# Three Strassen products in layer A: where the top-k rounds, the key and value splits, the next queries' load and the last rotation stand

## The chip, the cores and the metric

The kernel runs on one core of one Trainium2 chip. The metric is the device time of one execution, in microseconds; the time before is the median of three runs, 1827.25 us (1826.81 to 1828.52).

## The reference, cut to what matters

The reference is a decoder trunk of two layers over 512 positions of width 2048, in float32. Layer A is the one that the change touches:

```python
def mixer_a(x, w_in, w_o, positions):
    proj = x @ w_in
    q, k, v, gate, iq, ik, iw = jnp.split(proj, SPLITS_A, axis=-1)
    q = partial_rope(q.reshape(b, s, N_HEADS_A, HEAD_DIM), positions, ROT_DIM)
    k = partial_rope(k.reshape(b, s, N_KV_A, HEAD_DIM), positions, ROT_DIM)
...
    def block_fn(args):
        dots = jnp.einsum('bqhd,bsd->bqhs', iqb, ik)
        iscore = jnp.einsum('bqhs,bqh->bqs', jax.nn.relu(dots), iwb) * idx_scale
        iscore = jnp.where(causal[None], iscore, -jnp.inf)
        _, idx = lax.top_k(iscore, n_sel)
        ksel = jax.vmap(lambda kk, ii: kk[ii])(k, idx)
        vsel = jax.vmap(lambda vv, ii: vv[ii])(v, idx)
        logits = jnp.einsum('bqngd,bqknd->bqngk', qg, ksel) * (HEAD_DIM ** -0.5)
        wts = jax.nn.softmax(logits, axis=-1)
        o = jnp.einsum('bqngk,bqknd->bqngd', wts, vsel)
...
    return (o * jax.nn.silu(gate)) @ w_o
```

There are 16 query heads of width 128 in four groups, each group sharing one key and value head. An indexer scores all earlier positions for each query, and the attention sees only the 128 best of them (n_sel is min(256, 512 / 4)). Layer B is a stick-breaking attention over keys and values that are computed once. After each layer come a layer norm and a gated embedding.

## The kernel before, in words

Everything is kept transposed: a tile has 128 features on the partitions and positions along the free axis. Every float32 product is three matmuls (lines 147 to 149, `mm3`): each operand is split into a high part, rounded to the matmul's own format, and a low part that holds the rest. `split` makes them: ScalarE copies the high part (`wh`, `sh`, `xh`, `qh`, `kh`, `vh`, `ph`), VectorE subtracts for the low part (`wl`, `sl`, and so on). A weight streams from memory into a raw tile, is split, and is then read by TensorE. Buffers for parts are few (three each of wh, wl, sh and sl), so both engines work a few products ahead of TensorE and no further.

Some products are done by Strassen's scheme with seven products instead of eight. Their weights need sums of quarters, which VectorE adds before the split. The seven results stand in seven of the eight PSUM banks, and `combine` puts them together: ScalarE copies one into `u` and two more into the result, VectorE adds the rest. The next pass begins in the free bank and then needs the others one by one, so TensorE waits if `combine` empties them late.

Layer A runs in this order. First come the indexer's queries and keys and the query groups 0 to 2, with the indexer's scores between them. Then come the keys and values, in three stages of products (m2 and m4; m1 and m7; m6, m5 and m3). Then come three Strassen passes (`n` is 0, 1 and 2): the gates of groups 1 and 2 and the queries of group 3. While the second pass runs, `turn_keys` transposes the keys on TensorE. Last comes attention: four head groups `g`, each in four blocks `i` of 128 queries, beside the plain products of the gates of groups 0 and 3, whose steps fill TensorE's time between the blocks' own matmuls.

The order of work is written out by hand in three ways.

- `bg` is a queue of small pieces of work, above all for VectorE. `pumped` and `pumped_at` take one piece from it at chosen steps of a product. In the order of VectorE's instructions it stands at that place.
- Top-k is done in rounds of VectorE: `more` finds the eight largest values of a row (MAX8) and replaces them (MATCH_REPLACE8); sixteen rounds find 128, and a `mask` of two operations then turns the rest into additive masks `am`. For the last block of queries five pieces are still undone when the indexer's scores are through: four rounds and the mask. They are taken off `bg` into the list `rounds` (line 1067) and put back in the second Strassen pass (line 1134).
- In attention, `beside` (called with the strings in `ORDERS` and `OTHERS`) writes each block as letters: S is one head's scores and softmax of the next block, T four transposes of the probabilities, V the product with the values, f one step (three matmuls) of a gate product. The list `waiting` holds small pieces, and each f takes one from it (`one_waiting`), behind the newest exponential and the newest scaling of a softmax. Scores and transposes share three spare PSUM banks.

The tiles `F[0]` to `F[3]` hold the query groups and lend their room. When attention begins, `F[1]` holds the keys (`Kf`) and `F[2]` the values (`Vf`), while the queries of groups 1 and 2 wait in device memory (`held_q`). A load of group 1 into `F[1]` (line 1314) can start only when the last of the four `split_key` has read the keys, and the load into `F[2]` (line 1313) when the last `split_value` has read the values. Both are issued from GpSimd's queue, which works in order. The queries of group 1 are then split (`following_query`). Group 3 is finished by three sums of `combine` that are left over (`late`), by packing the rows to be rotated (`pack_rows`, four DMAs), and by the rotation itself (`turns`, four pieces of VectorE that end with four DMAs back).

Of the kernel before, what the change touches and what calls it, by code (L numbers as in the profile page):

```python
# [18 lines left out]
T = 512  # L19
# [32 lines left out]
def steps(gen, n):  # L52
    for _ in range(n):
        next(gen, None)
# [23 lines left out]
def trunk_kernel(  # L78
# [16 lines left out]
    nc = tc.nc  # L95
# [63 lines left out]
    F = [top.tile([128, 4, T], F32, name=f"f{c}") for c in range(4)]  # L159
# [251 lines left out]
    bg = deque()  # L411

    def paced(fn, *args):
        was, pinned[0] = pinned[0], True
        fn(*args)
        pinned[0] = was
# [409 lines left out]
    waiting = deque()  # L826
    held_g = {g: dram.tile([128, 4, T], F32, name=f"heldg{g}") for g in (1, 2)}
    held_q = [dram.tile([128, 4, T], F32, name=f"heldq{g}") for g in range(3)]
# [213 lines left out]
    def pair(first, name):  # L1042
        return [bank((first + j) % 8, name) for j in range(2)]
# [30 lines left out]
    for j in range(2):  # L1074
        paced(lambda: act.activation(c21[:, j], m4[j], AF.Copy, scale=-1.0))

    m1, m7 = pair(1, "m1"), pair(7, "m7")
    run(pumped(gemm_quarters(kv, ((half(0, 0), m1), (summed(1), m7))), 6))
    for j in range(2):
# [18 lines left out]
    steps(gemm, 2)  # L1098
    for j in range(2):
        paced(dve.tensor_tensor, u[:, j], u[:, j], m6[j], ALU.add)  # L1100
    steps(gemm, 2)
    for j in range(2):
        paced(act.activation, c12[:, j], m5[j], AF.Copy)
# [26 lines left out]
    for n, g in enumerate((1, 2, 3)):  # L1130
        M = product_banks(1 - n)
        gemm = pumped_at(gemm_s(items, C3A, M), PUMPS[n])
        if n == 1:
            bg.extend(rounds)
            steps(gemm, 40)
            for k in range(4):
                steps(gemm, 16)
                turn_keys(k)
        if n == 2:
            nc.gpsimd.dma_start(F[0][:, 0:2], held_q[0][:, 0:2])  # L1140
            bg.extend(turned_rows(KP, lambda g: key_rows(g, slice(0, 32))))
        run(gemm)
        drain()
        if n < 2:
            bg.extend(combine(None, M, lambda i: quarter(F[3], i), u[:, :, 0:H]))
            bg.extend(lambda j=j: act.activation(F[3][:, j], F[3][:, j], AF.Silu) for j in range(4))
            bg.append(lambda g=g: nc.gpsimd.dma_start(held_g[g], F[3]))
# [17 lines left out]
    def split_value(t):  # L1165
        split(*V[t], Vf[:, t])

    def split_key(g):
        split(*(k.rearrange("p (t s) -> p t s", t=4) for k in K[g]), key_rows(g))
# [14 lines left out]
    def following_query(g, h):  # L1184
        Q[g + 1, h] = split_query(g + 1, h)

    def scores(g, i):
        w = 128 * (i + 1)
        s = slice(i * 128, w)
        sm = pb.tile([128, 4, 4], F32, name="sm", tag="sm", bufs=2)  # L1190
        P[i] = pb.tile([128, 4, 384 + 128 * (i % 2)], F32, name="p", tag=f"p{i % 2}")
        for h in range(4):
            ps = spare("s")
            mm3(ps[:, :w], [q[:, s] for q in Q[g, h]], [k[:, :w] for k in K[g]], True, True)
            p = P[i][:, h, :w]
            least, rs, ri = (sm[:, h, j : j + 1] for j in range(3))
            with tc.issue_after(newest["soft" if h == 0 else "first"].ins) if "soft" in newest else ExitStack():
                newest["first"] = dve.tensor_tensor_reduce(p, ps[:, :w], am[i], -HSCALE, -GONE, ALU.add, ALU.min, least)
            newest["exp"] = act.activation(p, p, AF.Exp, bias=least, scale=-1.0, accum_out=rs)
            dve.reciprocal(ri, rs)  # L1200
            newest["soft"] = dve.tensor_scalar(p, p, ri, None, ALU.mult)
            if i == 3 and g < 3 and h == 3:
                if g == 1:
                    waiting.extend([lambda: None] * 5)
                waiting.extend(lambda h=h: following_query(g, h) for h in range(g == 1, 4))
            if (g, i, h) == (3, 3, 3):
                waiting.extend(lambda n=n: split(*plain(n), fblock(n)) for n in (0, 8, 1, 9))
            yield
            if i == 3 and g == 1 and h == 1:
                following_query(1, 0)  # L1210
# [61 lines left out]
    def beside(order, following, values):  # L1272
# [18 lines left out]
    OTHERS = {  # L1291
# [10 lines left out]
    def first_query(h):  # L1302
        Q[0, h] = split_query(0, h)

    for n, piece in enumerate((
        late.popleft(), late.popleft(), lambda: split_key(0), *(lambda h=h: first_query(h) for h in range(2)),
        lambda: split_value(0), *(lambda h=h: first_query(h) for h in range(2, 4)),
    )):
        steps(fill, 2 if n > 2 else 1)
        paced(piece)  # L1310
    waiting.extend((
        *late, lambda: split_value(1), lambda: split_key(1), lambda: split_value(2), lambda: split_key(2),
        lambda: split_value(3), lambda: nc.gpsimd.dma_start(F[2], held_q[2]), lambda: split_key(3),
        lambda: nc.gpsimd.dma_start(F[1], held_q[1]), pack_rows, *turns,
    ))
    first = scores(0, 0)
    beside("S f S f S f S fff", first, None)
# [939 lines left out]
```

## Time and profile before

| what | value |
|---|---|
| median of three runs | 1827.25 us |
| the profiled execution | 1829.19 us |
| its span, first to last instruction | 1827.1 us |
| TensorE busy | 1812.9 us, 99% of the span |
| VectorE busy | 1544.9 us, 85% |
| ScalarE busy | 1052.9 us, 58% |
| chain that ended last, share of TensorE | 96% |
| mean granted TensorE clock | 0.998 |

The table is from the page of the profiled execution. Busy time tells little here on where time is lost, since TensorE is busy nearly always; the views to read are the waits of TensorE (who waited for whom) and then the timeline around each of them. A wait for several things is put down to the one that came last. Times in a timeline count from the start of the span.

### The profile page before, as it was taken

The numbers are of one execution on the slowest core, as the hardware profiler recorded it, in microseconds if no ns is written. First come the engines' busy times: TensorE is split into PE (matmuls) and PEld (weight loads), VectorE is DVE, ScalarE is ACT, GpSimd is POOL, SyncE is SP. The second block draws the span as 40 slices with busy tenths as digits, with TensorE's granted clock in tenths as the row PEclk, the third lists the DMA queues.
The fourth block names the chain that finished last, engine by engine and source line by source line (L and its number), as shares of the span: only waits on it lengthen the run. The fifth ranks groups of instructions, "written<-read, shape, count | busy, mean of one in ns | idle before, by whom it ended". The sixth has DMA issues, their size and how long they took to land.

```text
span 1827.1 us, 28253 instructions
## 1 busy us (share of the span) xinstructions
PE 1812.9 (99%) x10231; PEld 1596.4 (87%) x10231; DVE 1544.9 (85%) x3085; ACT 1052.9 (58%) x1953; POOL 33.5 (2%) x75
## 2 busy tenths in 40 slices
PE   9999999999899999999999999999999999999999
PEld 8888888999788899888888899997888889988898
DVE  7888989988778899976568998888877889997997
ACT  4564355456566644575346444468888854557644
POOL 0001100001000000000000000000000000000000
PEclk9999999999999999999999999999999999999999
DMA  6524575345322344433437633322122244534453
GB/s 215 163 74 135 173 234 167 97 128 156 103 75 64 101 120 116 140 104 103 139 110 235 197 105 105 105 93 90 61 70 69 71 124 118 146 120 138 122 150 122
DMA packets 123740, 226.40 MB, mean 124 GB/s; under 512 B 10512, under 2 KB 40208, under 8 KB 122064
## 3 DMA queue, kind: packets, MB, share of 16 engines
q1 hardware_dynamic: 119936, 209.25, 38.3%
q0 software_dynamic: 3376, 14.95, 2.5%
q8 instruction: 80, 1.31, 0.3%
q14 instruction: 60, 0.49, 0.1%
q10 hardware_dynamic: 288, 0.39, 0.1%
HBM read 205.42 MB, written 16.78 MB: 122 GB/s over the span
## 4 chain that ended last, share of the span: by engine, by line
PE 96%; DVE 2%; DMA 1%; ACT 1%; issue 0%; POOL 0%; ACTq 0%; DVEq 0%; POOLq 0%
PE m L147 12%; PE m L149 12%; PE m L148 12%; PE g L147 10%; PE g L148 10%; PE g L149 10%; PE o L148 4%; PE o L149 4%; PE o L147 4%; PE q L149 2%; PE q L147 2%; PE q L148 2%; PE iq L149 1%; PE iq L147 1%; PE iq L148 1%; PE z L2050 1%
## 5 line engine op out<-in xcount | busy, mean ns | idle before, releaser
L118 ACT ACTIVATE wh<-raw 128x512 fp32r<-128x512 f32 (+3 forms) x561 | 309.3, 552 | 376.0 <-PE g L148 118.1
L118 DVE TENSOR_TENSOR wl<-raw,wh 128x512 fp32r<-128x512 f32 (+3 forms) x560 | 330.8, 592 | 112.2 <-ACT wh L118 106.2
L147 PE MATMUL g<-xh,wh 128*128 128x512 f32 (+1 forms) x816 | 317.9, 390 | 0.6 <-ACT Sq L118 0.6
L148 PE MATMUL g<-xl,wh 128*128 128x512 f32 (+1 forms) x816 | 314.8, 386 | 0.0
L149 PE MATMUL g<-xh,wl 128*128 128x512 f32 (+1 forms) x816 | 314.7, 386 | 0.0
L149 PEld LDWEIGHTS g<-xh,wl 128*128 128x128 f32 x816 | 153.4, 188 | 31.2
L147 PEld LDWEIGHTS g<-xh,wh 128*128 128x128 f32 x816 | 153.7, 188 | 30.1 <-ACT Sq L118 1.0
L148 PEld LDWEIGHTS g<-xl,wh 128*128 128x128 f32 x816 | 153.8, 188 | 28.5
L118 ACT ACTIVATE sh<-f 128x512 fp32r<-128x512 f32 x129 | 80.2, 624 | 105.6 <-DVE f L118 99.7
L147 PE MATMUL m<-xh,wh 128*128 128x256 f32 x400 | 113.4, 284 | 0.6 <-ACT u L118 0.6
L149 PE MATMUL m<-xh,wl 128*128 128x256 f32 x400 | 113.2, 283 | 0.0
L148 PE MATMUL m<-xl,wh 128*128 128x256 f32 x400 | 113.2, 283 | 0.0
L118 DVE TENSOR_TENSOR sl<-f,sh 128x512 fp32r<-128x512 f32 x129 | 88.8, 689 | 19.2 <-ACT sh L118 18.9
L147 PE MATMUL m<-c,sh 128*128 128x256 f32 x368 | 104.3, 283 | 0.0
L149 PE MATMUL m<-c,sl 128*128 128x256 f32 x368 | 104.3, 283 | 0.0
L148 PE MATMUL m<-c,sh 128*128 128x256 f32 x368 | 104.1, 283 | 0.0
L147 PE MATMUL o<-xh,wh 128*128 128x512 f32 x256 | 99.6, 389 | 0.0
L148 PE MATMUL o<-xl,wh 128*128 128x512 f32 x256 | 99.6, 389 | 0.0
L149 PE MATMUL o<-xh,wl 128*128 128x512 f32 x256 | 99.6, 389 | 0.0
L147 PE MATMUL m<-xh,sh 128*128 128x256 f32 x336 | 95.2, 283 | 0.0
L149 PE MATMUL m<-xh,sl 128*128 128x256 f32 x336 | 95.1, 283 | 0.0
L148 PE MATMUL m<-xl,sh 128*128 128x256 f32 x336 | 95.1, 283 | 0.0
(456 smaller groups left out, 4788.5 us busy)
## 6 DMA issues: line engine op xcount, KB each, us to landing
raw<-w_in_a SPq DMA_DIRECT2D x95, 512.0 KB, 3.8
raw<-w_in_b SPq DMA_DIRECT2D x64, 512.0 KB, 3.8
raw<-w_ple_gate SPq DMA_DIRECT2D x44, 512.0 KB, 4.0
raw<-w_o_a SPq DMA_DIRECT2D x24, 512.0 KB, 4.8
raw<-w_o_b SPq DMA_DIRECT2D x24, 512.0 KB, 4.7
f<-w_in_a SPq DMA_DIRECT2D x16, 512.0 KB, 4.7
f<-w_kv_b SPq DMA_DIRECT2D x16, 512.0 KB, 4.5
raw<-w_kv_b SPq DMA_DIRECT2D x16, 512.0 KB, 4.5
```

Of the source, the lines that this page charges most:

```text
L118: ins = method(*args, **kw)
L147: pe.matmul(out, a[0], b[0], start=start, stop=False)
L148: pe.matmul(out, a[0], b[1], start=False, stop=False)
L149: pe.matmul(out, a[1], b[0], start=False, stop=stop)
L2050: pe.matmul(z, down if kb % 2 else tri, p, start=False, stop=n == 1, skip_group_check=True)
```

## The change

Four things change in layer A; what is computed stays the same.

The five pieces in `rounds` are dealt out: two rounds are taken in the key and value product m1 and m7, one stands behind the sums with m6, and only the last round and the mask remain for the second Strassen pass. Value split 1 and key splits 1 and 2 are made while the gate product starts, ahead of the first scores. The list `waiting` then begins with key split 3 and the load of group 1's queries, and the load into `F[2]` follows the last value split. The late sums, the packing and the rotation of group 3 come only behind the queries of group 1, when the last scores of the first head group are written. And one f moves from the end of block (1, 1) to the end of block (1, 2).

```diff
+    bg.extend(rounds[:2])
     m1, m7 = pair(1, "m1"), pair(7, "m7")
     run(pumped(gemm_quarters(kv, ((half(0, 0), m1), (summed(1), m7))), 6))
...
         paced(dve.tensor_tensor, u[:, j], u[:, j], m6[j], ALU.add)
+    paced(rounds[2])
     steps(gemm, 2)
...
         if n == 1:
-            bg.extend(rounds)
+            bg.extend(rounds[3:])
             steps(gemm, 40)
...
                 waiting.extend(lambda h=h: following_query(g, h) for h in range(g == 1, 4))
+            if (g, i, h) == (0, 3, 3):
+                waiting.extend((*late, pack_rows, *[lambda: None] * 3, *turns))
...
-        (1, 2): "S T f S T f V S f T V S f V fff",
+        (1, 1): "S T f S T S f V S f V ff",
+        (1, 2): "S T f S T f V S f T V S f V ffff",
...
-    for n, piece in enumerate((
-        late.popleft(), late.popleft(), lambda: split_key(0), *(lambda h=h: first_query(h) for h in range(2)),
-        lambda: split_value(0), *(lambda h=h: first_query(h) for h in range(2, 4)),
-    )):
-        steps(fill, 2 if n > 2 else 1)
-        paced(piece)
+    for ahead, fn, n in (
+        (1, lambda _: late.popleft()(), 0), (1, lambda _: late.popleft()(), 0), (1, split_key, 0),
+        (2, first_query, 0), (2, first_query, 1), (2, split_value, 0), (1, split_value, 1), (1, first_query, 2),
+        (1, split_key, 1), (1, first_query, 3), (0, split_key, 2),
+    ):
+        steps(fill, ahead)
+        paced(fn, n)
     waiting.extend((
-        *late, lambda: split_value(1), lambda: split_key(1), lambda: split_value(2), lambda: split_key(2),
-        lambda: split_value(3), lambda: nc.gpsimd.dma_start(F[2], held_q[2]), lambda: split_key(3),
-        lambda: nc.gpsimd.dma_start(F[1], held_q[1]), pack_rows, *turns,
+        lambda: split_key(3), lambda: nc.gpsimd.dma_start(F[1], held_q[1]), lambda: split_value(2), lambda: None,
+        lambda: split_value(3), lambda: nc.gpsimd.dma_start(F[2], held_q[2]),
     ))
```

Block (1, 1) had no entry of its own before and took `"S T f S T S f V S f V fff"` from `ORDERS`.

Three places show how the instructions move. In the rows `f_109` to `f_112` are `F[0]` to `F[3]`, `am_128` to `am_131` the masks of the four query blocks.

The first place is VectorE at the end of the second Strassen pass, just ahead of `combine`, which begins with the row that writes `f_112` from a product bank. Before:

```order
L118 MAX m_2103<-wk 128x8
L118 MATCH_REPLACE wk<-m_2103,wk 128x512
L118 TENSOR_TENSOR f_109<-f_109,raw 128x2x128
L118 TENSOR_TENSOR f_109<-raw,f_109 128x2x128
L118 TENSOR_TENSOR wl<-raw,wh 128x384
L118 TENSOR_TENSOR sl<-f_109,sh 128x512
L118 TENSOR_TENSOR wl<-raw,wh 128x384
L118 TENSOR_TENSOR sl<-f_109,sh 128x512
L118 TENSOR_TENSOR am_131<-wk,am_131 128x512
L118 TENSOR_SCALAR am_131<-am_131 128x512
L118 TENSOR_TENSOR f_112<-m_3535,u 128x2x256
```

And the same place now:

```order
L118 TENSOR_TENSOR f_109<-f_109,raw 128x2x128
L118 TENSOR_TENSOR f_109<-raw,f_109 128x2x128
L118 TENSOR_TENSOR wl<-raw,wh 128x384
L118 TENSOR_TENSOR sl<-f_109,sh 128x512
L118 TENSOR_TENSOR wl<-raw,wh 128x384
L118 TENSOR_TENSOR sl<-f_109,sh 128x512
L118 TENSOR_TENSOR f_112<-m_3541,u 128x2x256
```

The last round in these rows and the mask are gone from ahead of `combine`; another round a little earlier is gone too.

The second place is VectorE between the last softmax of the first head group (`p` of 128x512) and the first scores of the second (`p,sm` with `am_128`). Before:

```order
L118 TENSOR_SCALAR p<-p,sm 128x512
L118 STREAM_SHUFFLE sw<-rp 128x512
L118 TENSOR_TENSOR sw<-sw,Sq 128x512
L118 TENSOR_TENSOR rp<-rp,Cq 128x512
L118 TENSOR_TENSOR ql<-f_110,qh 128x512
L118 TENSOR_TENSOR wl<-raw,wh 128x512
L118 TENSOR_TENSOR rp<-rp,sw 128x512
L118 ISA p,sm<-s,am_128 128x128
```

And now:

```order
L118 TENSOR_SCALAR p<-p,sm 128x512
L118 TENSOR_TENSOR f_112<-f_112,wk 128x2x256
L118 TENSOR_TENSOR ql<-f_110,qh 128x512 x4
L118 ISA p,sm<-s,am_128 128x128
L118 ISA sm 128x1
L118 TENSOR_TENSOR wl<-raw,wh 128x512
```

The rotation (shuffle, two products, sum) has left this place, one late sum has come, and all four query splits now stand ahead of the first scores, where only one stood before.

The third place is GpSimd's queue at the start of attention, from the keys' rotated rows to the rotated rows of group 3. Before:

```order
L986 DMA f_110<-rp 32x4x128 x4
L1176 DMA rp<-f_112 32x512 x4
L1313 DMA f_111<-heldq_142 128x2048
L1314 DMA f_110<-heldq_141 128x2048
L986 DMA f_112<-rp 32x512 x4
```

And now:

```order
L986 DMA f_110<-rp 32x4x128 x4
L1318 DMA f_110<-heldq_141 128x2048
L1319 DMA f_111<-heldq_142 128x2048
L1178 DMA rp<-f_112 32x512 x4
L986 DMA f_112<-rp 32x512 x4
```

The load of group 1's queries (`f_110`) has moved ahead of that of group 2, and both ahead of the packing of group 3's rows.

## The prediction

> **What bounds the kernel now.** I read the page's totals first, then TensorE's waits over the whole span, then the granted clock by stretches.
>
> ```profile
> PE 1812.9 (99%) x10231; PEld 1596.4 (87%) x10231; DVE 1544.9 (85%) x3085; ACT 1052.9 (58%) x1953; POOL 33.5 (2%) x75
> PE s L147 <- ACT qh L118: 2.7, 2, 1.8
> PE m L147 <- DVE f L118: 1.8, 1, 1.8
> PE s L147 <- DVE sm L118: 1.5, 1, 1.5
> PE s L149 <- DVE ql L118: 0.7, 2, 0.4
> PE m L147 <- ACT u L118: 0.6, 1, 0.6
> PE g L147 <- ACT Sq L118: 0.6, 1, 0.6
> 434.20:481.90 47.70, 43.35 (x216) 35.38 (x214) 41.48 (x116) 32.31 (x78) 3.73 (x8) 1.00 0.40 129
> 481.90:488.30 6.40, 5.87 (x21) 5.11 (x22) 4.07 (x13) 2.76 (x8) 1.39 (x3) 0.50 0.36 113
> 488.30:1828.00 1339.70, 1333.46 (x7523) 1171.52 (x7522) 1117.67 (x2182) 796.53 (x1466) 5.64 (x14) 1.00 0.38 113
> ```
>
> TensorE is the bound: it is busy 99% of the span, and no matmul is added or taken out. So the change can gain only what TensorE loses by waiting, and by running at half clock, as it did in one stretch of 6.40 us (column PEclk, third from the right: 0.50 there, 1.00 before and after). In the waits (total us, times, longest) all six rows lie between 390 and 523 us, and the edits lie in or just ahead of that stretch. They sum to 7.9 us. Half of the 5.87 us that TensorE was busy at clock 0.50 is 2.9 us. So about 11 us, 0.6% of the span, is all there is to win. After 523 us the trace shows TensorE no wait on which this change bears, so what is won there should reach the end.
>
> **Top-k rounds taken out of the second Strassen pass.** This is the end of that pass on TensorE, VectorE and ScalarE (start, duration, instruction, idle time before it):
>
> ```profile
> 391.62 0.39 PE L147 MATMUL m<-xh,wh 128*128 128x256 f32 x1 [0.64 <-ACT u L118]
> 394.08 0.39 PE L147 MATMUL m<-ca,sh 128*128 128x256 f32 x1 [1.84 <-DVE f L118]
> 394.88 0.39 PE L147 MATMUL m<-ca,sh 128*128 128x256 f32 x1 [0.17 <-DVE u L118]
> 384.50 0.68 DVE L118 MAX8 m<-wk 128x8 f32<-128x512 f32 x1
> 385.89 0.55 DVE L118 TENSOR_TENSOR wl<-raw,wh 128x384 fp32r<-128x384 f32 x1
> 391.68 0.68 DVE L118 TENSOR_TENSOR sl<-f,sh 128x512 fp32r<-128x512 f32 x1
> 392.28 0.69 DVE L118 TENSOR_TENSOR am<-wk,am 128x512 f32<-128x512 f32 x1
> 393.34 0.68 DVE L118 TENSOR_TENSOR f<-m,u 128x512 f32<-128x512 f32 x1
> 389.01 0.53 ACT L118 ACTIVATE wh<-raw 128x384 fp32r<-128x384 f32 x1
> 389.93 1.15 ACT L118 ACTIVATE sh<-f 128x512 fp32r<-128x512 f32 x2 [0.40 <-DVE f L118]
> 390.99 0.58 ACT L118 ACTIVATE u<-m 128x512 f32<-128x512 f32 x1
> ```
>
> TensorE waits for product banks that combine has to empty. A round costs VectorE 385.89 - 384.50 = 1.39 us and the mask 393.34 - 392.28 = 1.06 us. The change takes three rounds' worth out of the tail of the pass: two rounds go, the mask replaces a third, and the mask at the end goes, 2 x 1.39 + 0.33 + 1.06 = 4.2 us. That isn't the gain, since ScalarE is next in line: its wh at 389.01 follows the copies of turned keys without a gap, so its two sh can move up only by the 0.40 us that they waited for VectorE, and u to about 390.6. The second sl then runs near 391.2, and the add that empties the bank (393.34 before) at 391.8. TensorE restarts 1.5 us earlier. Bounds: 0.4 us, if only ScalarE's step counts, and 2.65 us, if all three waits go. I take 1.5.
>
> **The same rounds put in earlier.** Two go into the product pair m1 and m7 of the key and value weights, one just ahead of the first Strassen pass.
>
> ```profile
> 253.70:275.50 21.80, 21.80 (x98) 18.05 (x97) 16.91 (x28) 11.59 (x20) 0.00 (x0) 1.00 0.76 237
> 275.50:308.10 32.60, 32.60 (x145) 27.01 (x144) 29.86 (x51) 17.17 (x30) 0.00 (x0) 1.00 0.56 179
> 290.93 0.68 DVE L118 TENSOR_TENSOR sl<-t,sh 128x512 fp32r<-128x512 f32 x1
> 294.51 0.39 PE L147 MATMUL m<-sh,xh 128*128 128x512 f32 x1
> 341.53 0.69 DVE L118 TENSOR_TENSOR sl<-f,sh 128x512 fp32r<-128x512 f32 x1 [0.29 <-ACT sh L118]
> 344.34 0.28 PE L149 MATMUL m<-ca,sl 128*128 128x256 f32 x1
> 348.52 0.69 DVE L118 TENSOR_TENSOR u<-m,u 128x512 f32<-128x512 f32 x1
> 349.50 0.28 PE L147 MATMUL m<-ca,sh 128*128 128x256 f32 x1
> ```
>
> The first stretch is m1 and m7, where VectorE is idle 21.80 - 16.91 = 4.9 us; two rounds (2.8 us) fit in, though not all of the idle time lies behind them. I expect some 1.5 us of delay to be carried into the next stretch, where VectorE has only 2.7 us of idle time, most of it at the end. A weight part made there is used about 2.9 us after it is ready (ready at 291.61; the matmul at 294.51 is the start of the product that reads it, the fifteenth of 24), so nothing waits. In the first Strassen pass the third round delays VectorE by 1.39 us; its parts are ready 344.34 - 342.22 = 2.1 us before use in the tightest case, so again nothing waits. But at the end of that pass the banks are emptied with little room: the add to u ends at 349.21, and the matmul that needs its bank starts at 349.50, 0.3 us later. About 1 us of the delay is still there by then, so TensorE waits some 0.6 us that it doesn't wait now. Bounds: 0, and 1.4 us, the whole round. I take +0.6.
>
> **Key and value splits ahead of the scores, the late sums and the rotation behind them.** Value split 1 and key splits 1 and 2 now stand ahead of the first scores, and key split 3 and value split 2 soon after; in return three sums of the last query group leave that place.
>
> ```profile
> 443.55 1.28 ACT L118 ACT_TABLE_LOAD   x1
> 446.92 0.69 DVE L118 TENSOR_TENSOR f<-f,wk 128x512 f32<-128x512 f32 x1
> 457.37 0.69 DVE L118 TENSOR_TENSOR kl<-f,kh 128x512 fp32r<-128x512 f32 x1
> 459.38 0.69 DVE L118 TENSOR_TENSOR pl<-pt,ph 128x512 fp32r<-128x512 f32 x1
> 460.22 0.41 PE L147 MATMUL s<-kh,qh 128*128 128x384 f32 x1 [1.47 <-DVE sm L118]
> ```
>
> These are ScalarE's table load and one of the three sums at the first scores, and three rows at the scores of the third query block. The scores at 460.22 wait for a spare bank that the pl at 459.38 gives back. Just ahead of that pl stand two kl (one is shown) and two vl, 0.6 us from start to start like 391.68 and 392.28 above; afterwards one vl stands there, so pl comes 1.8 us earlier and the wait of 1.47 us goes whole. At the early place VectorE gets five splits for three sums, 1.2 us more. ScalarE's table load there (1.28 us, ahead of the first exponential) moves behind one more split, and VectorE uses the time it idled for it; I find the fourth softmax of the first block ready within 0.1 us of where it is. So the early place costs 0; its bound is those 1.2 us. I take -1.5.
>
> **The next queries' load first.** Here lies the largest term. The queue's load of F[1], ScalarE's first split of it, and TensorE's two longest waits for it:
>
> ```profile
> 470.42 0.55 POOL L1314 DMA_DIRECT2D f<-heldq  x1 [3.12 <-DVE kl L118]
> 478.45 0.63 ACT L118 ACTIVATE qh<-f 128x512 fp32r<-128x512 f32 x1 [3.10 <-DMA f<-heldq]
> 479.14 0.33 PE L147 MATMUL s<-kh,qh 128*128 128x128 f32 x1 [1.77 <-ACT qh L118]
> 482.32 0.48 PE L147 MATMUL s<-kh,qh 128*128 128x128 f32 x1 [0.97 <-ACT qh L118]
> ```
>
> The load takes 478.45 - 470.42 = 8.0 us and its own row names what it waited for, the last key split (kl), which reads F[1]. Key split 3 now stands where the sums stood (446.92), and the load stands ahead of F[2]'s on GpSimd's queue, so it starts near 447 and lands near 455, some 20 us before its first reader. What is next: the four query splits run one behind the other right after the last softmax of the block, with one late sum ahead, 5 x 0.6 = 3.0 us of VectorE, during which TensorE has the gate matmuls and its first transposes; the first scores' bank is freed just about when the second transposes want it. I leave 0.5 us for that. The rows of waits on qh and ql (2.7 + 0.7 = 3.4 us) go, and with them, I think, the half clock behind them, 2.9 us: -3.4 - 2.9 + 0.5 = -5.8. [...]
>
> **One gate step dealt from the end of the block (1, 1) to the end of (1, 2).**
>
> ```profile
> 522.40 0.50 PE L147 MATMUL g<-xh,wh 128*128 128x512 f32 x1 [0.59 <-ACT Sq L118]
> ```
>
> This wait is for ScalarE's gate evacuation, which stands behind the last exponential of (1, 2). One step (three matmuls) more behind those scores covers it: -0.6. The block (1, 1) ends with one step less, as (0, 1) does already without a wait at its end. The rotation moved into this group adds four VectorE operations of 0.6 us. VectorE's idle time hides them (behind 488.3 us it is busy 1117.67 of 1339.70 us, five sixths); uncovered, they'd cost 2.4 us.
>
> **Sum.** -1.5 + 0.6 - 1.5 - 5.8 - 0.6 = -8.8 us. A matmul that restarts after a wait takes 0.39 us where the same form takes 0.28 (394.08 against 349.50), 0.1 us for each of seven waits, -0.7; for small new waits I add 0.5. That is -9.0 us. The profiled execution took 1829.19 us (1827.1 of span and 2.1 around it), so it would take 1820.2. The median of the runs shown is 1827.25, 1.9 below it; from that the forecast is 1818.2 us.
>
> **The rivals.**
> The stall moves: the four splits and the late sum hold back the first scores' softmax, and TensorE waits about 1.2 us twice where it waits 3.4 now, close enough together for half clock again. That costs 2.4 + 2.9 = 5.3 us against 6.3 now, so 1.0 of the 5.8 us is left: -4.2, 1823.0 us. For it speaks that VectorE is busy 41.48 of 47.70 us in that stretch; against it, that ScalarE stood idle there for 3.10 us for nothing but the load. Chance 0.13.
> The clock stays low although the waits go, because something other than these waits lowers it in that stretch: -9.0 + 2.9 = -6.1, 1821.1 us. For it: the waits of 391 us, in sum as long, lowered nothing. Against it: the only half clock stands right behind the densest group of waits. [...] Chance 0.07.
> The early rounds cost more: VectorE is nearly full from 275 to 308 us, and if the 1.2 us of delay carried in find no room there and the third round comes through whole at 349 us (1.4 instead of 0.6), 2.0 us come back: -7.0, 1820.2 us. Chance 0.14.
> The load isn't early after all, because on GpSimd's queue another step still holds it: only -1.5 + 0.6 - 1.5 - 0.6 = -3.0 is left, 1824.2 us. Against it: its row (470.42) names only the key split. Chance 0.06.
> Slower: the shuffle of the last rotation now stands among the scores of the second group, and VectorE works in order, so if the packed rows land later than the scores need it, all softmax work stands behind it. The rows are now issued behind both large loads on the same queue; if both were still under way, they would land 2 x 8.0 = 16 us after their issue, of which some 5 us are covered by the work between. TensorE would stand 11 us and then run at half clock once more: -9.0 + 11 + 2.9 = +4.9, 1832.1 us. It decides at 5 us from issue to landing. Against it: the loads start near 447 and 456 us, some 25 us ahead, and three empty turns stand between issue and shuffle. Chance 0.04.
> The forecast has the rest, 0.56.
>
> **How the numbers follow.** The forecast's own bounds (term one by +1.1 or -1.1, term two by -0.6 or +0.8, the early splits by 1.2, the rotation) give about 1815 to 1820.5. The range takes in all rivals down to a gain of 4.2 and leaves out the load that isn't early and the slower case: 1815.0 to 1823.0. A measurement of this kernel can tell about 0.2% from no change, 3.7 us. Faster by more than that are the forecast and the first three rivals, 0.56 + 0.13 + 0.07 + 0.14 = 0.90, less 0.04 for rivals that come together: 0.86. Within it, the load that isn't early, a quarter of the slower case (only one load ahead) and those 0.04: 0.11. Slower, 0.03.
>
> **What would show it.** In the profile after: no wait of scores for qh or ql near 477 us and clock 1.00 throughout; the wait for sm near 460 gone; near 391 a wait for f of about 0.5 to 1 us left; a new wait of about half a microsecond near 349; no wait for Sq near 515. The forecast is wrong if a wait on DVE or ACT of over 1 us stands in the first scores of the second group, or if TensorE waits between 260 and 345 us.

## The result and the profile after

| | before | after |
|---|---|---|
| median of four runs | 1827.88 us (1826.81 to 1829.38) | 1817.86 us (1817.29 to 1819.04) |
| ratio, 95% interval | | 0.9945 (0.9928 to 0.9963) |
| the profiled execution: time, span | 1829.19, 1827.1 us | 1817.29, 1815.2 us |

The whole interval lies under 0.998, so the kernel is faster by more than the 0.2% that a measurement of it can tell. The forecast was 1818.2 us. The size is right; the experiments show that the reason given for the largest term was not, so the fit of the sum is in part luck.

TensorE's waits of after over the whole span (total us, times, longest), and two of the stretches shown of before:

```profile
PE 1808.2 (100%) x10231; PEld 1594.3 (88%) x10231; DVE 1543.9 (85%) x3085; ACT 1051.1 (58%) x1953; POOL 33.6 (2%) x75
PE spun L167 <- PEq L2253: 0.8, 1, 0.8
PE m L147 <- DVE f L118: 0.8, 1, 0.8
PE m L147 <- DVE u L118: 0.4, 2, 0.2
PE pt L1225 <- DVE p L118: 0.3, 1, 0.3
PE iq L147 <- ACT wh L118: 0.2, 1, 0.2
434.20:481.90 47.70, 47.44 (x248) 39.99 (x247) 43.65 (x128) 35.83 (x87) 2.80 (x6) 1.00 0.40 128
481.90:488.30 6.40, 6.40 (x36) 5.48 (x35) 4.54 (x18) 3.41 (x9) 0.34 (x1) 1.00 0.36 105
```

All waits for qh, ql, sm and Sq are gone, and the clock is 1.00 in both stretches (and from 488.30 us to the last matmul). What is left among the old waits stands near 391 us. The end of both Strassen passes on TensorE, VectorE and ScalarE:

```profile
349.56 0.39 PE L147 MATMUL m<-ca,sh 128*128 128x256 f32 x1 [0.18 <-DVE u L118]
392.65 0.39 PE L147 MATMUL m<-ca,sh 128*128 128x256 f32 x1 [0.77 <-DVE f L118]
391.91 0.68 DVE L118 TENSOR_TENSOR f<-m,u 128x512 f32<-128x512 f32 x1
387.93 0.60 ACT L118 ACTIVATE f<-kt 128x512 f32<-128x512 f32 x1 [2.19 <-PE kt L1121]
389.58 1.14 ACT L118 ACTIVATE sh<-f 128x512 fp32r<-128x512 f32 x2
390.63 0.58 ACT L118 ACTIVATE u<-m 128x512 f32<-128x512 f32 x1
```

The bank is emptied at 391.91 us (391.8 was forecast) and TensorE goes on at 392.65 (1.5 us earlier than 394.08 was forecast). ScalarE is indeed next in line: its two sh and its u run in one row up to that add. It had idled 2.19 us for the last transposed keys (kt) just before. The small new wait of the prediction is at 349.56.

GpSimd's queue, ScalarE's query splits and VectorE's shuffle of after:

```profile
445.95 0.57 POOL L1318 DMA_DIRECT2D f<-heldq  x1 [15.32 <-DVE sm L118]
473.39 1.02 POOL L1178 DMA_DIRECT2D rp<-f  x2 [17.85 <-DVE f L118]
481.25 0.99 POOL L1178 DMA_DIRECT2D rp<-f  x2 [6.85 <-DVE sm L118]
471.69 2.18 ACT L118 ACTIVATE qh<-f 128x512 fp32r<-128x512 f32 x4
484.61 0.74 DVE L118 STREAM_SHUFFLE sw<-rp 128x512 f32<-128x512 f32 x1
```

The load of F[1] is issued at 445.95 us (about 447 was forecast), some 26 us ahead of its first reader. The four splits run in one row at 471.69. The shuffle has no idle time ahead of it (it would stand in brackets), so the packed rows were there.

To put a price on each place I took, for every matmul, how much later than usual it starts after the one before it (usual: the median spacing of the same two forms in that trace), and summed this by stretches. For before there are three traces, two of them from the last experiment below, so differences of a few tenths are scatter:

| stretch, us | before, three traces | after | forecast of the difference |
|---|---|---|---|
| 250 to 360 | -0.1, -0.1, -0.1 | 1.0 | +0.6 |
| 380 to 400 | 3.6, 5.1, 5.1 | 2.0 | -1.5 |
| 440 to 458 | 0.9, 0.9, 0.9 | 1.1 | 0 |
| 458 to 470 | 2.0, 2.0, 2.0 | 0.4 | -1.5 |
| 470 to 495 | 7.8, 6.3, 7.6 | 1.0 | -5.8 |
| 508 to 530 | 1.55, 1.64, 1.58 | 0.93 | -0.6 |
| the whole span | 22.0, 21.5, 23.0 | 11.5 | -9.0 |

### The profile page after: what moved, and what is told of

The parts are those of the page before. It is cut to its first block, busy times and chain, and to the rows that moved or that the text cites. A ratio compares the mean times of both kernels' runs of the same rounds, so it can differ in the third digit from the quotient of the medians.

```text
span 1815.2 us, 28253 instructions
## 1 busy us (share of the span) xinstructions
PE 1808.2 (100%) x10231; PEld 1594.3 (88%) x10231; DVE 1543.9 (85%) x3085; ACT 1051.1 (58%) x1953; POOL 33.6 (2%) x75
## 4 chain that ended last, share of the span: by engine, by line
PE 97%; DVE 1%; ACT 1%; issue 0%; DMA 0%; ACTq 0%; DVEq 0%
PE m L147 12%; PE m L148 12%; PE m L149 12%; PE g L147 10%; PE g L148 10%; PE g L149 10%; PE o L148 4%; PE o L149 4%; PE o L147 4%; PE q L149 2%; PE q L148 2%; PE q L147 2%; PE iq L149 1%; PE iq L147 1%; PE iq L148 1%; PE z L2055 1%
## 5 line engine op out<-in xcount | busy, mean ns | idle before, releaser
L118 DVE TENSOR_TENSOR sl<-f,sh 128x512 fp32r<-128x512 f32 x129 | 88.8, 689 | 22.2 <-ACT sh L118 22.1
```

What stands on the lines that cost most here:

```text
L118: ins = method(*args, **kw)
```

## The experiments

Medians are given with the ratio to runs of the kernel before on the same chip (1827.46, 1827.27 and 1827.01 us in the three sessions).

### Is it the load?

The load alone, in the kernel before (key splits 2 and 3 come ahead of value splits 2 and 3 with it, since the load can start only behind the last key split):

```
-        *late, lambda: split_value(1), lambda: split_key(1), lambda: split_value(2), lambda: split_key(2),
-        lambda: split_value(3), lambda: nc.gpsimd.dma_start(F[2], held_q[2]), lambda: split_key(3),
-        lambda: nc.gpsimd.dma_start(F[1], held_q[1]), pack_rows, *turns,
+        *late, lambda: split_value(1), lambda: split_key(1), lambda: split_key(2), lambda: split_key(3),
+        lambda: nc.gpsimd.dma_start(F[1], held_q[1]), lambda: split_value(2), lambda: split_value(3),
+        lambda: nc.gpsimd.dma_start(F[2], held_q[2]), pack_rows, *turns,
```

> The kernel before, with one part of the change alone: key split 3 and the load of F[1] ahead of value splits 2 and 3 and of the load of F[2]; sums, rounds, rotation and gate steps stay as before. My theory, that the largest term lies here: the waits for qh and ql near 479 us (3.4 us in all) go and the half clock behind them goes with them, 5.8 us less than before (about 1822.1 against 1827.9), a ratio of 0.997, while the waits for f near 394, sm near 460 and Sq near 522 stay. Rival 'the clock stays low': the waits go, a stretch of about 6 us at clock 0.50 stays, 2.9 us less (1825.0). Rival 'the stall moves': new waits on VectorE in the first scores of the second group, 1 us less.

Measured: 1827.35 us, ratio 0.9999 (0.9990 to 1.0007): no gain that can be told from noise, where 5.8 us were expected; the interval leaves room for 1.8 us at most. (In its trace the stretch from 470 to 495 us loses some 5 us by the table's measure, 1 to 3 less than in the three of before.) GpSimd's queue, ScalarE's query splits, two of VectorE's steps of the rotation, and TensorE's waits in this run:

```profile
460.96 0.58 POOL L1313 DMA_DIRECT2D f<-heldq  x1 [7.66 <-DVE kl L118]
477.41 0.62 ACT L118 ACTIVATE qh<-f 128x512 fp32r<-128x512 f32 x1
481.92 0.61 ACT L118 ACTIVATE qh<-f 128x512 fp32r<-128x512 f32 x1
484.83 0.61 ACT L118 ACTIVATE qh<-f 128x512 fp32r<-128x512 f32 x1
488.84 0.62 ACT L118 ACTIVATE qh<-f 128x512 fp32r<-128x512 f32 x1
478.15 0.76 DVE L118 STREAM_SHUFFLE sw<-rp 128x512 f32<-128x512 f32 x1
481.39 0.69 DVE L118 TENSOR_TENSOR rp<-rp,sw 128x512 f32<-128x512 f32 x1
482.58 0.33 PE L147 MATMUL s<-kh,qh 128*128 128x128 f32 x1 [1.12 <-ACT qh L118]
483.73 0.33 PE L149 MATMUL s<-kh,ql 128*128 128x128 f32 x1 [0.71 <-DVE ql L118]
```

The load is early (460.96 instead of 470.42), and no query split waits for a DMA any more. But the four splits stand 3 to 4.5 us apart, not in a row as in after: each gate step takes one piece off the list `waiting`, and the pieces of the last rotation stand in it ahead of the query splits, so that splits two to four are taken only among the next group's scores. The same pieces stood there in the trace of before, the last of them behind the first query split (ql at 479.12):

```profile
475.51 0.73 DVE L118 STREAM_SHUFFLE sw<-rp 128x512 f32<-128x512 f32 x1
480.33 0.69 DVE L118 TENSOR_TENSOR rp<-rp,sw 128x512 f32<-128x512 f32 x1
```

So two causes stood one behind the other, the late load and the rotation's pieces, and the load's lateness only hid the second. The old theory, that the load is the term, fell here. The rotation alone, then the two together (in the kernel before):

```
-        ... pack_rows, *turns,
+            if (g, i, h) == (0, 3, 3):
+                waiting.extend((pack_rows, *[lambda: None] * 3, *turns))
```

> The kernel before, with the packing of rows and the last rotation moved behind the next queries' splits, as in after, and the load of F[1] left where it was, last of the loads. New theory (from the run with the early load alone, where the time stayed and waits of 1.1 + 1.1 us and about 3.4 us of half clock were left): two causes stand one behind the other, the late load and the rotation's VectorE steps, which are dealt one a turn ahead of query splits two to four; each alone covers the other. Then here the first wait (1.8 us, for the load) stays, the ones behind it (1.0 us at 482, 0.4 at 490) go, and of the half clock some may stay: 1.3 us less than before if all of it stays, 4 us less if it goes. Old theory (the load alone makes the stall): no change.

Measured: 1824.40 us, ratio 0.9980 (0.9971 to 0.9989), 2.9 us less. The first wait, which was expected to stay, went too: ScalarE's splits of this run,

```profile
478.83 1.67 ACT L118 ACTIVATE qh<-f 128x512 fp32r<-128x512 f32 x3 [0.94 <-DMA f<-heldq]
480.93 0.61 ACT L118 ACTIVATE qh<-f 128x512 fp32r<-128x512 f32 x1
```

wait only 0.94 us for the load, since it took 5.9 us here (issued at 472.94) instead of 8.0; TensorE waits 0.15 us, and the clock at 470 to 495 us stays 1.00.

> The kernel before, with both: the load of F[1] early and the rotation behind the next queries' splits; rounds, sums, early splits and gate steps as before. New theory: no wait for qh or ql near 480 us and clock 1.00 there, 5 to 6.3 us less than before (about 1821.7, ratio 0.997), with the waits near 391, 460 and 522 still there. Rival: the early key and value splits are needed as well, so that a wait on VectorE stays in the first scores of the second group; under 3 us less.

Measured: 1822.57 us, ratio 0.9971 (0.9959 to 0.9982), 4.7 us less where 5 to 6.3 were expected; no wait for qh or ql, clock 1.00 from 400 us on, and the waits for f (1.8), sm (1.5), u and Sq (0.6 each) are all still there. So of 4.7 us the rotation's place brings 2.9 by itself, the load's place by itself nothing that the medians show, and 1.8 us on top of the other; the intervals of the last two runs overlap, so that 1.8 is no more than likely.

One experiment missed its aim. To hold the load back in after, I put it behind F[2]'s load and five empty turns:

```
-        lambda: split_key(3), lambda: nc.gpsimd.dma_start(F[1], held_q[1]), lambda: split_value(2), lambda: None,
-        lambda: split_value(3), lambda: nc.gpsimd.dma_start(F[2], held_q[2]),
+        lambda: split_key(3), lambda: split_value(2), lambda: None, lambda: split_value(3),
+        lambda: nc.gpsimd.dma_start(F[2], held_q[2]), *[lambda: None] * 5, lambda: nc.gpsimd.dma_start(F[1], held_q[1]),
```

> The kernel after, with the load of F[1] alone put back, behind F[2]'s and five empty turns, to about the 470 us where it stood before; the key split ahead of it stays early. My theory, that TensorE's waits bring the half clock: waits for qh and ql of 3 to 4 us come back near 477 us and with them some 6 us at clock 0.50, 5 to 6.5 us more than after (about 1823.5 against 1817.9). Rival 'the clock is lowered by something else' (here by what stood around it before): the waits come back, the clock stays at 1.00, 3 us more (1821). If the load is hidden anyway: no wait and 0 us.

Measured: 1817.48 us, as after. In the list F[1]'s load now stands last, but in the trace it is still issued first, where after has it (445.95 there):

```profile
446.71 0.57 POOL L1319 DMA_DIRECT2D f<-heldq  x1 [15.32 <-DVE sm L118]
454.50 0.56 POOL L1319 DMA_DIRECT2D f<-heldq  x1 [7.21 <-DVE sm L118]
```

The first row is F[1]'s load, since it comes right behind the last key split (done at 446.42 us); the second comes behind the last value split (done at 454.20), which F[2]'s load has to wait for. So empty turns hold no load here, and what fixes its time is the key split that reads F[1] before it. The run says nothing on the stall.

### The top-k rounds

The rounds alone, in the kernel before, and the rounds put back, in after (the same three lines the other way round):

```
+    bg.extend(rounds[:2])
+    paced(rounds[2])
-            bg.extend(rounds)
+            bg.extend(rounds[3:])
```

> The kernel before, with the top-k rounds alone dealt as the change deals them (two into m1 and m7, one behind the sums of m6, the rest and the mask as before). My theory: -1.5 us near 391 and +0.6 us near 349, 0.9 us less than before, which the time can hardly show (ratio 0.9995); in the trace TensorE's waits at 391 to 395 fall from 2.65 us to about 1 us, and about 0.5 us of late matmuls stands near 349. Rival 'the early rounds cost more': waits between 275 and 310 us and 1.4 us near 349, time the same as before or up to 0.5 us more. Everything from 440 us on is as before, the half clock with it.

Measured: 1830.03 us, ratio 1.0013 (1.0004 to 1.0022), 2.6 us more than before, where 0.9 less was expected.

> The kernel after, with the top-k rounds put back to the second Strassen pass. If the deal of the rounds is worth what the trace of after shows (waits near 391 of 0.8 instead of 2.5 us, and 0.7 us of late matmuls near 349): 1 to 1.5 us more than after (1819.1), with waits for f of 1.8 and u of 0.6 near 392 and none near 349. Rival, from the run with the rounds alone, which took 2.4 us longer than before: the deal costs time in itself, and this kernel is as fast as after or 1 to 2 us faster. My theory is the first: in that run the time was lost in the stall at 480 us, which is not there in after.

Measured: 1819.33 us (1819.27 to 1820.71), ratio 0.9955 (0.9942 to 0.9968), 1.5 us more than after and without overlap with its runs, as the first theory has it. TensorE's waits of this run at the end of the second pass:

```profile
392.11 0.39 PE L147 MATMUL m<-xh,wh 128*128 128x256 f32 x1 [0.66 <-ACT u L118]
394.57 0.39 PE L147 MATMUL m<-ca,sh 128*128 128x256 f32 x1 [1.83 <-DVE f L118]
```

So the deal is worth 1.5 us where nothing stalls behind it, and cost 2.6 us where the stall at 480 us was still there. In that stall the trace of the rounds alone shows more loss than before (8.7 us at 470 to 495 against 7.8, 6.3 and 7.6): TensorE comes earlier to a load that doesn't (issued at 470.74 us here, 470.42 in before). A second trace of the same kernel:

> The kernel before with the top-k rounds alone dealt, for a second trace of it, to see why it takes 2.4 us longer than before. Theory: with the waits at 391 us gone, TensorE comes 1.6 us earlier to the stall at 480 us, which is as long as the load makes it; its windows there are busy 0.46, far under the edge, so half clock comes for two windows in every execution, while in the kernel before it is at the edge (0.565) and comes in some. Then here too: two windows of half clock near 481 to 488 us. Rival: the second trace has none or one, and the 2.4 us come from elsewhere.

Measured: 9.3 us of loss at 470 to 495. Half clock lasts for whole windows of 3.41 us in these traces (6.82 us in the first, 10.24 in the second), more on which under "When the clock halves". The window ahead of the half clock and the half clock itself, in the first trace and in the second (stretch, its us, TensorE's busy us, and PEclk third from the right):

```profile
477.53:480.95 3.42, 1.57 (x10) 1.31 (x10) 1.88 (x4) 1.40 (x3) 0.00 (x0) 1.00 0.01 5
480.95:487.77 6.82, 4.97 (x16) 3.67 (x15) 5.40 (x16) 3.49 (x9) 1.99 (x4) 0.50 0.42 115
```

```profile
475.06:478.48 3.42, 1.50 (x7) 0.86 (x5) 0.46 (x2) 1.09 (x2) 0.00 (x0) 1.00 0.15 63
478.48:488.72 10.24, 9.06 (x31) 7.35 (x31) 7.38 (x20) 4.05 (x11) 1.99 (x4) 0.50 0.26 77
```

Two windows of half clock in the one and three in the other; the kernel before has two, none and two in its three traces. That fits, but the traces alone can't show it: in total the traced executions of the two kernels lose the same (22.5 and 22.1 us against 22.0, 21.5 and 23.0), and those of before took 1828.0 to 1829.3 us, above its median. The mean granted clock is on record for the runs without a trace too: it is 0.997 or 0.998 in all eleven runs of the rounds alone, and 0.996 to 1.000 in the 21 of before beside them, 0.999 or more in twelve. On average that is 0.9977 against 0.9986; an estimate from the two and the span of 1827 us gives 1.5 us. So more than half of the 2.6 us is half clock that before has only in some of its executions; the rest stays open.

### The gate step

```
-        (1, 1): "S T f S T S f V S f V ff",
-        (1, 2): "S T f S T f V S f T V S f V ffff",
+        (1, 2): "S T f S T f V S f T V S f V fff",
```

> The kernel after, with the gate step of (1, 2) put back to the end of (1, 1). My theory: the wait for ScalarE's gate evacuation, 0.6 us behind the scores of (1, 2) near 511 us, comes back, 0.6 us more than after, which only the trace can show. Rival: the wait was there because ScalarE was late from the stall at 479 to 490 us, and doesn't come back now that this stall is gone: 0 us, no wait.

Measured: 1818.60 us, ratio 0.9954 (0.9942 to 0.9966), 0.7 more than after. The runs of the two overlap, so the time alone doesn't show it, but in the trace the wait is back, behind the scores of (1, 2):

```profile
513.73 0.50 PE L147 MATMUL g<-xh,wh 128*128 128x512 f32 x1 [0.57 <-ACT Sq L118]
```

### What is left near 391 us

The transposes of keys earlier, first with the third round in m1 and m7 as well, then alone (in after):

```
-    bg.extend(rounds[:2])
+    bg.extend(rounds[:3])
-    paced(rounds[2])
-            steps(gemm, 40)
+            steps(gemm, 34)
```

> The kernel after, with the third round dealt into m1 and m7 too (instead of behind m6's sums), and the four transposes of keys six steps earlier in the second Strassen pass. Theory: the rest of the waits near 391 us (0.8 us for f, some 1.8 us of late matmuls in all) is ScalarE's, which idles 2.2 us for the last transposed keys and then has copies, weight parts and u in one row; six steps earlier (2.3 us) take 1 us or more of it away; and the 0.7 us near 349 go with the third round: 1.5 us less than after (1816.3). Rival: three rounds are too many for VectorE between 275 and 310 us, new waits of 0.5 us or more there or at 349: no gain.

Measured: 1816.62 us, ratio 0.9936 (0.9923 to 0.9949), 1.2 us less than after. The waits at 391 and 349 us are gone, but the rival is right as well, a new one stands at 279 us:

```profile
279.39 0.50 PE L147 MATMUL m<-sh,xh 128*128 128x512 f32 x1 [1.43 <-ACT f L118]
```

ScalarE's copy that this matmul waits for is late behind a wait of 1.73 us for VectorE (to 277.19 us), and VectorE has no idle time there. The last two lines of that diff alone:

> The kernel after, with the four transposes of keys six steps earlier in the second Strassen pass and nothing else. In the run that also moved the third round, the waits near 391 us were gone, and a wait of 1.4 us for a bank had come near 277 us. Theory, that the transposes alone did the first and the third round the second: waits near 391 gone, 0.7 us of late matmuls near 349 as in after, 0.3 us near 277; 1.7 us less than after, 1816.1 (0.5 less than the run with both). Rival, that the third round in m1 and m7 helped at 391 too: the wait for f there stays at 0.5 us or more.

Measured: 1815.13 us (1814.82 to 1815.79), ratio 0.9933 (0.9919 to 0.9946), the fastest of all, 2.7 us less than after where 1.7 was expected. None of its five runs overlaps with those of after (1817.29 to 1819.04), but they are from another session, and the intervals of the two ratios overlap. Its waits over the whole span, and ScalarE at the end of the second pass:

```profile
PE spun L167 <- PEq L2253: 0.8, 1, 0.8
PE pt L1225 <- DVE p L118: 0.3, 1, 0.3
PE m L147 <- DVE u L118: 0.2, 1, 0.2
385.50 0.60 ACT L118 ACTIVATE f<-kt 128x512 f32<-128x512 f32 x1 [0.41 <-PE kt L1121]
388.98 0.57 ACT L118 ACTIVATE u<-m 128x512 f32<-128x512 f32 x1
```

ScalarE idles 0.41 instead of 2.19 us for the keys, its copy to u comes at 388.98 instead of 390.63, and nothing waits at 391 us. So the keys' place did this, and the third round is best left where the change put it.

### When the clock halves

The kernel before, unchanged, twice more.

> The kernel before, unchanged, for a second trace of it. In the ten traces so far the stretches of half clock begin and end at whole multiples of 3.41 us after TensorE's clock was first full; they follow each window of that grid in which TensorE was busy for 0.565 or less and no window with 0.566 or more. The grid lies elsewhere in each execution. Theory: the same waits near 391 us (2.65 us in all) and 480 us (3.4 us) bring half clock or not according to where the grid cuts them, so this trace may have it at both places, at one, or at none; wherever a window is busy under 0.56 it does, and where it is over 0.58 it doesn't. Rival, which the prediction held: half clock follows the density of waits, so it stands behind the waits at 480 us alone, as in the first trace.

> The same once more, a third trace of the kernel before: the same expectations as of the second.

Measured: 1828.02 and 1829.32 us. The stretches of half clock within the program are 3.41, 6.83 or 10.24 us long in these traces and in those above, one to three times 3.41 us; in the third trace of before the two begin at 395.26 and 480.59 us, 25 times 3.41 us apart. Call the steps of 3.41 us, counted from the start of such a stretch, the grid and each step a window. These are the windows about the two stalls and what follows them (stretch, its us, TensorE's busy us, and PEclk third from the right), first in the trace shown of before, then in the second and the third:

```profile
389.54:392.96 3.42, 2.06 (x16) 1.65 (x14) 3.19 (x6) 3.02 (x6) 0.00 (x0) 1.00 0.44 153
392.96:396.37 3.41, 2.11 (x15) 1.91 (x16) 3.27 (x8) 0.00 (x0) 0.00 (x0) 1.00 0.49 153
457.81:461.22 3.41, 1.94 (x12) 1.64 (x11) 3.41 (x11) 2.25 (x7) 0.00 (x0) 1.00 0.02 6
478.29:481.70 3.41, 1.93 (x10) 1.31 (x10) 2.42 (x6) 2.10 (x6) 0.40 (x1) 1.00 0.10 11
481.70:488.53 6.83, 6.10 (x21) 5.34 (x22) 4.33 (x14) 3.09 (x9) 1.59 (x4) 0.50 0.37 110
```

```profile
390.75:394.16 3.41, 1.41 (x7) 0.99 (x8) 3.27 (x7) 1.34 (x3) 0.00 (x0) 1.00 0.55 157
394.16:397.58 3.42, 3.42 (x17) 3.42 (x18) 3.10 (x8) 1.48 (x3) 0.00 (x0) 0.50 0.00 1
479.50:482.91 3.41, 2.15 (x12) 1.50 (x12) 3.22 (x9) 1.88 (x5) 1.35 (x3) 1.00 0.31 76
```

```profile
391.84:395.26 3.42, 1.75 (x12) 1.54 (x13) 3.28 (x7) 0.38 (x1) 0.00 (x0) 1.00 0.52 156
395.26:398.67 3.41, 3.41 (x18) 3.41 (x18) 3.09 (x8) 1.56 (x3) 0.00 (x0) 0.50 0.00 0
477.18:480.59 3.41, 1.54 (x8) 0.89 (x6) 2.05 (x4) 1.15 (x2) 0.00 (x0) 1.00 0.03 12
480.59:487.42 6.83, 6.33 (x20) 4.91 (x21) 4.96 (x15) 3.52 (x9) 1.99 (x4) 0.50 0.39 115
```

In the first trace the grid cuts the stall near 391 us in two (busy 2.06 and 2.11 of 3.41 us) and no half clock follows; in the other two it falls mostly into one window (1.41, 1.75), and half clock follows. At 480 us it is the other way round in the second trace: 2.15 us busy, and the clock stays (the mean granted clock of that trace is 0.999, of the others 0.998 and 0.997). The theory held at every window shown; the rival, that half clock stands behind the waits at 480 us alone and those at 391 us halve nothing, is wrong. Other columns don't tell the windows apart: 12 matmuls and 1.54 us of weight loads (the column behind) were followed by half clock at 391.84 us of the third trace, 12 matmuls and 1.50 us were not at 479.50 of the second. Nor does the longest gap: the waits of 1.12 and 0.71 us in the run with the load alone, in one window, were followed by half clock, the single wait of 1.47 us for sm (in the window from 457.81 us of the first trace) was not.

## Why the prediction was right, and where it was wrong

**The bound** was right. TensorE was the bound, and everything won came from its waits and its clock; after leaves it 2.5 us of waits in all, 1.3 of them at the start of the program and in places the change doesn't touch.

**Rounds taken out of the second Strassen pass** (-1.5): right in mechanism, and in size for the waits themselves. The add that empties the bank came at 391.91 for 391.8, and putting the rounds back cost 1.5 us. What the step left out is the clock. It took the first trace, where the waits at 391 us halved nothing, for how the kernel behaves; in the seven traces with the rounds in that pass (before three times, the load alone, the rotation alone, both, the rounds put back) half clock follows there in six, and the first was the exception. In the seven with the rounds dealt out it follows in none (in after, the rounds alone and the gate step put back the clock is 1.00 from 390 to 404 us). A window at clock 0.50 with TensorE busy throughout costs half of 3.41 us, 1.7, by an estimate from the clock column (in the trace of before the matmuls of 128x512 start 0.43 us apart at 485 to 486 us, at clock 0.50, and 0.23 us apart at 489, at 1.00). So by the three traces of before this term is -1.5 to -3.1, as the table's 3.6 and 5.1 against 2.0 show.

**The same rounds put in earlier** (+0.6): 0.7 us at 340 to 360 us, the small wait for u at 349.56 among it. That nothing would wait between 260 and 345 us was a little off: 0.3 us of late matmuls stand there. With a third round in m1 and m7 a wait of 1.43 us came there, so VectorE's room was used up, as the rival of the dearer early rounds had it, but one round later.

**Key and value splits early, late sums moved** (-1.5): -1.6 at 458 to 470 us, +0.2 at the early place. With both other edits of this stretch made but not this one, the wait for sm is still 1.5 us, so the term is this edit's.

**The next queries' load first** (-5.8): this step failed in its cause, not in its size. The stretch lost 5.3 to 6.8 us less, but the load alone brought nothing that its runs could tell (0.9999). The sentence that failed is "the four query splits run one behind the other right after the last softmax": it was put down to the early load, while it is the rotation's move that lets them. The row on which the step rested, ScalarE's 3.10 us for the load, names what came last, and says nothing of what stands one step behind it. The rotation's own steps in that stretch (a shuffle, three products or sums, one a turn, at 475.51, 476.28, 476.89 and 480.33 us in the trace of before) could have been seen, and the prediction priced their move as a cost only ("adds four VectorE operations"), where by itself it brought 2.9 of the 4.7 us that both bring. That the term came out all the same is luck: the move stood in the same change, and the prediction counted no gain for it. Right were the early issue, the free queue, and that no wait takes the place of the old ones: the 0.5 us left for that wasn't needed.

**The half clock** there (-2.9) went, but the prediction had only half of its cause, the waits that stand close together. It matters as much where the grid cuts them: the windows of layer A that half clock followed had TensorE busy for 0.92 to 1.93 of 3.41 us, the five shown that it did not follow for 1.93 to 2.15. The grid lies elsewhere in each of the three traces of before (near 391 us a window ends at 392.96, 394.16 and 395.26), and there this stall is followed by two windows of half clock, none and two, so the 2.9 us was one draw.

**The gate step** (-0.6): right, -0.6 to -0.7 by the table, and the wait of 0.57 us came back in the run that undid it.

**The sum** was -9.0 and the medians give -10.0, the profiled executions -11.9. By the table the known stretches give 1.1 - 1.6 + 0.2 - 1.6 - 6.8 - 0.6 = -9.3 against the first trace. Of the rest of 11.9, 0.9 stands at the start of the program, which no edit touches (the first 60 us lose 1.7 there against 0.8 after, and 0.8 and 1.1 in the other traces of before); where the remaining 1.7 lies was not traced.

**The rivals.** In after the stall didn't move, the clock didn't stay low, and the load was early. The slower case didn't come: the packed rows landed 1.9 us (median) after their issue at 473.39 and 481.25, and the shuffle at 484.61 found them.

## What to carry to other kernels

A wait's releaser is the one that came last; before a gain is put down to it, list what else stands between the waiting instruction and its start, and ask of each step that a change moves away from there what it had held up. When two causes stand in series, undoing one alone may show nothing (the load, here): make both runs and the pair. Time won ahead of a stall that a transfer sets can be lost in the stall; and one trace's clock is one draw, so take two or three before a term rests on it.

## What the runs showed of the hardware

The stretches of half clock within the program are 3.41 to 3.42 us long (from 394.16 us in the second trace of before, 395.26 in the third, 395.56 in the rotation alone), 6.82 to 6.83 (from 481.70 in the first trace of before, 480.59 in the third, 480.95 in the rounds alone) or 10.24 (from 478.48 in the second trace of the rounds alone). In eleven windows within layer A that were each followed by half clock TensorE was busy for 0.92 us (the rotation alone, from 392.15) to 1.93 us (before, from 478.29); in five that were not, for 1.93 us (the rotation alone, from 460.42) to 2.15 us (the second trace of before, from 479.50). At 1.93 us both were seen, so no exact edge is shown. Two of the five hold the wait for sm of 1.5 us, and in before, the load alone and the rounds alone, which all have that wait, the clock is 1.00 from 434 to 470 us. In the first trace of before the window at half clock from 481.70 us, busy for 2.68 us, was followed by another, the one from 485.12, busy throughout, by full clock. The same stall can thus cost nothing more than itself, or 1.5 us on top, by where the grid cuts it: at 380 to 400 us the table has 3.6 us for the first trace of before, with no half clock there, and 5.1 for the other two, with one window of it each. How the clock comes to be lowered no run shows. A matmul that restarts after a wait shows a longer busy time than the same one in a dense row (0.39 us against 0.28, at 394.08 and 349.50 in the trace of before), and their ends are modelled, so the busy times are not exact.

The load of F[1], 1 MB on GpSimd's queue, took 8.0 us from issue to landing in before and 5.9 in the run with the rotation alone; with the rounds alone the split that waited for it started 7.7 us after its issue (470.74 and 478.41). In these three it was issued 3.7 to 3.9 us behind the load of F[2] on the same queue, while that one was still under way (F[2]'s took 7.3 us in before; the median of the two loads is 6.5 us in the rotation alone and 7.9 in the rounds alone). Ahead of F[2]'s it took 5.0 us in after and 5.1 in the run with the load alone. So its early place also made it shorter. That the other load is the reason isn't shown: F[2]'s load took 7.2 and 5.1 us in those two, where it was issued (at 454.97 and 473.04) after F[1]'s had landed.
